# Retention and HGRN2 step on one core: low parts of W_out's B11 behind a scan's update, one scan step a product later, 17 small matmuls made twice

## The chip, the cores and the metric

The kernel runs on one core of a Trainium2 chip. The metric is the device time of one execution in microseconds (us); several runs are given by their median. One further execution was taken with a profile; all rows below are of that one.

The engines are called as the profile calls them: PE is TensorE's array and PEld its weight loads, DVE is VectorE, ACT is ScalarE, POOL is GpSimd, SP is SyncE (here it issues DMAs only). A matmul's output lies in PSUM; every other tile lies in SBUF.

## The reference, cut to what matters

One layer with two groups of four heads on the same normalised input of 2048 tokens by 1024 features: retention with a fixed decay for each head, and HGRN2, whose decay differs for each token and feature. Both are recurrences, taken in chunks; the outputs are gated and go together through one projection. Eight further tokens are decoded beside it.

```python
h = rmsnorm(x, norm_g)
p = (h @ w_in).astype(jnp.float32)
rq, rk, rv, rg, hq, hf, hi, hgate = jnp.split(p, 8, axis=-1)
...
# HGRN2: S_t = diag(f_t) S_{t-1} + k_t v_t^T, o_t = S_t^T q_t
b = jnp.cumsum(gc, axis=2)
o_inter = jnp.einsum('bhtd,bhdv->bhtv', qc * jnp.exp(b), S)
A = jnp.einsum('bhtd,bhsd,bhtsd->bhts', qc, kc, decay)
o = o_inter + jnp.einsum('bhts,bhsv->bhtv', A, vc)
...
o_cat = jnp.concatenate([o_ret, o_hg], axis=-1).astype(x.dtype)
y = x + o_cat @ w_out
```

The matrix `A` is the part that the change touches: its decay differs for each pair of tokens and each feature, so it isn't one product of q and k with a scalar in front.

## The kernel before

**Projections.** The products with W_in and W_out are cut into units, u from -6 to 31: values first (below 0), then W_in for queries, keys, forget gates and output gates (0 to 23), then W_out (24 to 31). By a scheme of Strassen's kind each unit is seven products of blocks (named by the operand of x: B11, T1, T2, B22, B21, T3, T4; operands of the weights are A11, S1 and so on), and each product is two halves of six matmuls, 128x512, at reduced precision: each operand is split into a high and a low part, and three of the four combinations are made. The high part is a rounding copy on ACT (`x_hi`, L743), the low part a subtraction on DVE (`x_lo`, L747), both over half of a block at a time; for x they are made once and kept for all units of the same half of the tokens. From unit 12 on the names begin with x1, for W_out with wo.

**Scans.** Units go round H (HGRN2: forget gates and queries), G (gates), R (retention: keys and queries). When a head's queries and forget gates are there, its scan is made beside the matmuls of the next units: unit 3's scan beside units 4 to 6, unit 9's beside units 10 and 11, unit 21's beside units 22 and 23. `A` is made by levels of a binary tree over the tokens. The steps `s0`, `s1`, `s2`, `s3` make the scores of one to two levels each, as runs of 32 fp32 matmuls of 32x16 (`small`, L1269; the first step also 32 of 32x32, L1287; the last step 16 of 32x32 and 16 of 32x64, L1321 and L1330). Between them DVE multiplies the keys and queries by the decay of a level (`update`: kh at L1234, then qth at L1237), and ACT copies them for the next step (`keep`: qh<-kh at L1248, fh<-qth at L1249), so that a step can make one level from the copies and the next level from the updated tiles. DVE puts the scores of the lower levels under a mask into fh (`put`, L1275); after the last step ACT copies the scores plh out of PSUM into A (L1340, L1342) and those of fh too (L1346). Then TensorE transposes the keys (pkh, L1085) and ACT copies them (ksh, L1091). The tiles pah, plh and pkh share one pool of two PSUM buffers: pkh's two groups take the buffers in which the last step's scores lay.

An fp32 matmul is two passes through the array, each with a weight load; so one fp32 matmul of a scan is four instructions of TensorE, and a 128x512 matmul of a product is two. `dec_mm(u)` (L809) are 16 fp32 matmuls for the decoded tokens on the weights of unit u.

**Order.** Nothing is reordered when the program is built: PE, DVE, ACT, POOL and SP each run their instructions in the order in which the code issues them. That order is set by an event list: `at(pos, f)` puts a piece of work at a position, where unit u's products stand at 7u and its next six slots, and the list is worked off by position. The table `AT` holds the offsets: `hgrn` for the scan's steps, `hd` for corrections to the steps of single scans (one tuple for each scan, offsets for s0 to s3), `swap` and `swapo` for the splits of x and of the operands of W_out, with four positions for each block (high and low part of its first half, then of its second). `wu` is the number of 32x8 matmuls on ones at the very start, ahead of the first product, which fill the time until its inputs have come.

## Time and profile before

| | us |
|---|---|
| median of 3 runs | 995.23 |
| the runs | 995.17, 995.23, 996.35 |
| the profiled execution | 994.56 |
| its span on the core | 992.8 |
| PE busy | 978.9 (99%) |
| DVE busy | 779.6 (79%) |
| ACT busy | 575.5 (58%) |
| POOL busy | 252.5 (25%) |
| mean DMA rate | 246 GB/s |

The span goes from the first to the last instruction on the core; 1.8 us of the execution's time lie around it. Busy times of engines overlap. An idle time in the profile is put down to what ended it: another engine's instruction, a DMA, or "issue", where the engine waited for nothing that the profile shows. TensorE's matmuls are pipelined, so that the starts of two matmuls lie closer together than one of them lasts. Runs of like instructions are given as one row with their count, and their passes are counted one by one. [...]

### The profile page before, as it was taken

How to read it: one execution, taken by the hardware profiler on the slowest of the kernel's cores; microseconds unless marked ns; L12 is line 12 of the kernel's file. 1: busy time of each engine (PE TensorE's matmuls, PEld its weight loads, DVE VectorE, ACT ScalarE, POOL GpSimd, SP SyncE). 2: the span in 40 equal slices, each digit the busy share in tenths (PEclk: the TensorE clock that was granted, in tenths of full speed). 3: DMA queues.
4: the chain of work that ended last, by engine and by line, in shares of the span. 5: the costliest groups of instructions: out<-in, count | busy, mean ns of one | idle time of the engine just before them, and what ended most of it. 6: DMA issues, size and time to landing. Idle time of an engine off the chain costs nothing. (4 is left out here: it accounts for less than half of the span.)

```text
span 992.8 us, 22960 instructions
## 1 busy us (share of the span) xinstructions
PE 978.9 (99%) x8831; PEld 815.9 (82%) x8831; DVE 779.6 (79%) x1355; ACT 575.5 (58%) x1348; POOL 252.5 (25%) x404
## 2 busy tenths in 40 slices
PE   9999999999999999999999999999999999999997
PEld 7788888888878887888888888888888878878886
DVE  6967696888778888878898766877867799867774
ACT  7855524856656664765885555456467577524332
POOL 1421231111332342232022222222237202312121
PEclk9999999999999999999999999999999999999999
DMA  9756669748868987784986993994996497784522
GB/s 310 239 182 245 223 218 360 291 154 301 261 194 279 300 284 266 269 273 159 354 277 187 320 307 121 317 303 130 317 333 215 156 362 275 244 267 156 212 85 85
DMA packets 121820, 244.05 MB, mean 246 GB/s; under 512 B 12600, under 2 KB 53184, under 8 KB 119024
## 3 DMA queue, kind: packets, MB, share of 16 engines
q1 hardware_dynamic: 98544, 164.69, 50.9%
q0 software_dynamic: 22880, 77.65, 21.1%
q8 instruction: 69, 1.13, 0.5%
q14 instruction: 39, 0.32, 0.1%
q10 hardware_dynamic: 288, 0.27, 0.1%
HBM read 155.97 MB, written 89.72 MB: 247 GB/s over the span
## 5 line engine op out<-in xcount | busy, mean ns | idle before, releaser
L1248 ACT ACTIVATE qh<-kh 128x1024 f32<-128x1024 f32 x24 | 25.5, 1062 | 46.3 <-DVE kh L1234 46.2
L1671 ACT ACTIVATE yj<-xro 128x512 f32<-128x512 f32 (+1 forms) x25 | 15.6, 624 | 60.3 <-DVE xro L750 42.7
L1234 DVE TENSOR_TENSOR kh<-kh,fph 128x512 f32<-128x512 f32 x48 | 33.0, 687 | 13.6 <-PE plh L1269 10.9
L1128 ACT ACTIVATE obh<-poh 128x128 f32<-128x128 f32 x64 | 16.9, 290 | 29.3 <-PE poh L1124 29.3
L1237 DVE TENSOR_TENSOR qth<-qth,fph 128x512 f32<-128x512 f32 x48 | 32.8, 683 | 0.0
L1128 ACT ACTIVATE obr<-por 128x128 f32<-128x128 f32 x64 | 16.8, 276 | 27.1 <-PE por L1124 27.1
L373 POOL TENSOR_TENSOR ms<-ms 128x2 f32<-128x2 f32 x8 | 10.0, 1255 | 86.5 <-ACT xn L369 86.5
L1689 DVE SCALAR_TENSOR_TENSOR xro<-xro,yms,fg 128x1024 f32<-128x1024 f32 (+1 forms) x16 | 20.0, 1247 | 13.5 <-POOL yms L1686 13.5
L1152 POOL DMA_DIRECT2D o_dram<-gtr x16 | 12.3, 769 | 67.5 <-DVE gtr L1149 20.8
L948 ACT ACTIVATE vo<-aV 128x512 f32<-128x512 f32 x12 | 7.1, 589 | 37.7 <-PE aV L918 37.7
L750 DVE TENSOR_TENSOR xro<-aO,xro 128x512 f32<-128x512 f32 (+1 forms) x33 | 22.2, 676 | 7.2 <-PE aO L918 7.1
L1152 POOL DMA_DIRECT2D o_dram<-gth x16 | 12.5, 778 | 57.5 <-DVE gth L1149 15.9
L265 POOL TENSOR_SCALAR orsh<-omsh 128x4 f32<-128x4 f32 x16 | 5.6, 347 | 83.3 <-ACT obh L1128 82.9
L1136 ACT ACTIVATE obh<-poh,orsh 128x128 f32<-128x128 f32 x64 | 18.2, 370 | 14.2 <-POOL orsh L266 14.2
L1115 DVE SCALAR_TENSOR_TENSOR sth<-sth,fph,puh 128x128 f32<-128x128 f32 x48 | 16.7, 347 | 10.3 <-PE poh L1124 7.8
L1122 PE MATMUL poh<-vh,A 128*128 128x128 f32 x128 | 24.0, 274 | 0.0
L1122 PE MATMUL por<-vr,A 128*128 128x128 f32 x128 | 24.0, 274 | 0.0
L1002 POOL DMA_DIRECT2D g_dram<-g x29 | 15.8, 546 | 27.8 <-DVE g L998 25.6
L1124 PE MATMUL por<-str,qr 128*128 128x128 f32 x112 | 21.8, 276 | 0.3 <-DVE str L1113 0.3
L369 ACT ACTIVATE xn<-xn 128x512 f32<-128x512 f32 x32 | 19.8, 622 | 3.5 <-DMA xn<-in_x_prompt 3.5
L1136 ACT ACTIVATE obr<-por,orsr 128x128 f32<-128x128 f32 x64 | 18.2, 368 | 6.1 <-POOL orsr L266 6.1
L1124 PE MATMUL poh<-sth,qth 128*128 128x128 f32 x112 | 21.7, 275 | 0.0
(1727 smaller groups left out, 3716.7 us busy)
## 6 DMA issues: line engine op xcount, KB each, us to landing
xn<-in_x_prompt SPq DMA_DIRECT2D x32, 256.0 KB, 4.4
v_dram<-vo SPq DMA_DIRECT2D x32, 256.0 KB, 2.4
xro<-in_x_prompt SPq DMA_DIRECT2D x16, 512.0 KB, 5.1
out_y_prompt<-xro POOLq DMA_DIRECT2D x15, 512.0 KB, 4.0
g_dram<-g POOLq DMA_DIRECT2D x29, 256.0 KB, 5.8
xr<-in_x_t SPq DMA_DIRECT2D x12, 512.0 KB, 6.2
vh<-v_dram SPq DMA_DIRECT2D x16, 256.0 KB, 8.8
gth<-g_dram SPq DMA_DIRECT2D x16, 256.0 KB, 6.7
```

Source lines behind the costliest of these rows:

```text
L369: act.activation(r, r, AF.Square, accum_out=ms[:, 2 * h + j : 2 * h + j + 1])
L750: dve.tensor_tensor(o, x, y, op=ALU.add)
L1115: dve.scalar_tensor_tensor(dst, src, decay(c), pu[:, j], op0=ALU.mult, op1=ALU.add)
L1122: pe.matmul(po[:, j], s_ctx["A"][:, c], box["v"][g][:, j], start=True, stop=src is None)
L1124: pe.matmul(po[:, j], qcol(c), src, start=False, stop=True)
L1128: act.activation(ob[:, j], po[:, j], AF.Square, accum_out=ms[:, j : j + 1])
L1136: act.activation(ob[:, j], po[:, j], AF.Copy, scale=rs[:, j : j + 1])
L1152: after(AT["gate"]["tr"], lambda: pool.dma_start(o_dram[c0 : c0 + 4, ty, :, h].rearrange("c p t -> p c t"), gt.rearrange("p (c t) -> p c t ...
L1234: dve.tensor_tensor(kv[:, :, 0, :], kv[:, :, 0, :], two[:, :, 1:2].to_broadcast([P, nb, b]), op=ALU.mult)
L1237: dve.tensor_tensor(qv[:, :, 1, :], qv[:, :, 1, :], two[:, :, 0:1].to_broadcast([P, nb, b]), op=ALU.mult)
L1248: act.activation(kept_k, k, AF.Copy)
L1689: dve.scalar_tensor_tensor(x[:, cc], x[:, cc], ms[:, 0:1], fg[:, cc], op0=ALU.mult, op1=ALU.mult)
```

## The change

Four things are edited.

- `swapo`'s B11, operand of W_out: high and low part of its second half stand 0.8 positions later. This moves them beside the scan of unit 21, behind its third step.
- `hd[3]`, the scan of unit 9: its third step `s2` stands a full position later, its last step `s3` 0.6 later. The third step now comes behind the product with B22 (eR<-x0B22) rather than ahead of it, and the last step between the two halves of the product with T3 (aR<-x0T3) rather than ahead of both.
- `wu`: 30 instead of 35; and `again`: after its 32 matmuls a scan step makes the first few again, with the same operands into the same place: 2 and 1 in the scan of unit 9 (s0, s2), 4 in unit 12's, 1 in unit 15's, 9 in unit 18's, 17 in all.
- `dec_mm(6)` stands just behind the third step of unit 3's scan, where it stood just ahead of it. Nothing else in TensorE's order there moves.

```diff
--- before.py
+++ after.py
@@ -115,7 +115,7 @@
            'lB21': 6.9,
            'lT3': 8.4,
            'lT4': 12.2,
-           'B11': (3.5, 3.5, 3.5, 3.5),
+           'B11': (3.5, 3.5, 4.3, 4.3),
            'T1': (6.5, 6.5, 7.0, 7.0),
            'T2': (8.2, 8.2, 8.7, 8.7),
            'B22': (8.9, 8.95, 9.2, 9.75),
@@ -126,7 +126,8 @@
  'x1s': (0.5, 1.8, 1.9, 3.4, 5.0),
  'wo': (26.9, 71.0, 101.8, 122.8),
  'wos': (0.0, 2.3, 3.3),
- 'wu': 35,
+ 'wu': 30,
+ 'again': {(3, 's0'): 2, (3, 's2'): 1, (4, 's2'): 4, (5, 's1'): 1, (6, 's2'): 9},
  'wop': (140.0, 2.133, 2.1, 2.833),
  'gate': {'G': 0.95, 'store': 1.6, 'R': 0.8, 'H': 0.7, 'root': 0.5, 'scale': 1.15, 'gt': 1.2, 'tr': 0.6},
  'fin': 1.0,
@@ -142,7 +143,7 @@
          'fin': 25.2},
  'dh': ((12.15, 14.75), (17.55, 20.15), (27.15, 28.65)),
  'dhs': (-5.0, -2.2, -2.2, -1.5),
- 'hd': ((0.0, 0.0, 0.0, 0.0), (0.0, 0.0, -0.5, -0.5), (0.0, 0.0, 0.0, 0.0), (0.3, 0.0, 0.0, 0.0),
+ 'hd': ((0.0, 0.0, 0.0, 0.0), (0.0, 0.0, -0.5, -0.5), (0.0, 0.0, 0.0, 0.0), (0.3, 0.0, 1.0, 0.6),
         (0.0, 0.0, 0.0, 0.0), (0.0, 0.5, 0.0, 0.0), (0.0, 0.0, 0.0, 0.0), (0.0, 0.0, 0.0, 0.5)),
  'retL': {'load': 12.0,
           's': 11.55,
@@ -831,8 +832,8 @@
         for n, name in enumerate(("A11", "S3", "A22", "A12")):
             at(U + {0: -7.6, 1: -8.6}.get(u, AT["w24"][0] if u == 24 else w["load"] if u % 3 or u >= 12 else w["load0"]) + 0.5 * n, lambda name=name: w_load(u, name))
         if u < 12:
-            if u == 3:
-                at(AT["hgrn"]["s2"] + AT["hd"][0][2] + 0.01, lambda: dec_mm(u))
+            if u in (3, 6):
+                at(7 * (u - 3) + AT["hgrn"]["s2"] + AT["hd"][u // 3 - 1][2] + 0.01, lambda: dec_mm(u))
             else:
                 at(U + d["mm" if u % 3 or not u else "mm0"], lambda: dec_mm(u))
             at(U + (-0.65 if u < 2 else d["copy" if u % 3 else "copy0"]), lambda: dec_copy(u))
@@ -1253,20 +1254,23 @@
             after(0.35, copies)
             after(1.1, lambda: update(li))
 
-        def small(dst, li, kept=False):
+        def small(dst, li, kept=False, again=0):
             b = LEVELS[li]
             m = 32 // (2 * b)
-            for c in range(CH):
-                for i in range(4):
-                    at_ = c * P + 32 * i
-                    if not kept:
-                        kk = k[:, at_ : at_ + 32]
-                        n0 = (c * 4 + i) * m
-                        qq = views(b)[0][:, n0 : n0 + m, 1, :]
-                    else:
-                        kk = kept_k[:, at_ : at_ + 32]
-                        qq = kept_q[:, at_ // 2 : at_ // 2 + 16]
-                    pe.matmul(dst[32 * i : 32 * i + 32, c], kk, qq, start=True, stop=True)
+            for n in range(4 * CH + again):
+                c, i = divmod(n % (4 * CH), 4)
+                at_ = c * P + 32 * i
+                if not kept:
+                    kk = k[:, at_ : at_ + 32]
+                    n0 = (c * 4 + i) * m
+                    qq = views(b)[0][:, n0 : n0 + m, 1, :]
+                else:
+                    kk = kept_k[:, at_ : at_ + 32]
+                    qq = kept_q[:, at_ // 2 : at_ // 2 + 16]
+                pe.matmul(dst[32 * i : 32 * i + 32, c], kk, qq, start=True, stop=True)
+
+        def more(step):
+            return AT["again"].get((u // 3, step), 0)
 
         def put(src, li):
             b = LEVELS[li]
@@ -1285,7 +1289,7 @@
                 for i in range(4):
                     cc = slice(c * P + 32 * i, c * P + 32 * i + 32)
                     pe.matmul(pd[32 * i : 32 * i + 32, c], k[:, cc], q[:, cc], start=True, stop=True)
-            small(p0, 0)
+            small(p0, 0, again=more("s0"))
             update(0)
             products(0, 1)
             keep(1)
@@ -1300,7 +1304,7 @@
         def scores(li):
             pl = ps_lv.tile([P, 2, CH, 16], F32, tag="lv", name=f"pl{name}{li}")
             small(pl[:, 0], li, True)
-            small(pl[:, 1], li + 1)
+            small(pl[:, 1], li + 1, again=more("s1" if li == 1 else "s2"))
             update(li + 1)
             keep(li + 2)
```

The order that comes of it, first on ACT beside the scan of unit 9. kh and qth are the scan's keys and queries, kr a tile of keys of the retention unit beside it (sw and big take its halves crosswise), x1T1l and x1T1h the low and high part of T1 of the second half of the tokens. Before:

```order
L1248 ACTIVATE qh_4783<-kh_4983 128x1024
L1249 ACTIVATE fh_4744<-qth_5117 128x512
L1009 ACTIVATE sw_5676<-kr_5406 64x512
L1010 ACTIVATE sw_5676<-kr_5406 64x512
L743 ACTIVATE x1T1h<-x1T1l 128x1024
L1340 ACTIVATE A<-plh_5681 32x4x32 x4
L1342 ACTIVATE A<-plh_5682 64x4x64 x2
L1346 ACTIVATE A<-fh_4744 32x8x32 x4
L743 ACTIVATE x1T1h<-x1T1l 128x1024
L1009 ACTIVATE big<-kr_5406 64x512
L1010 ACTIVATE big<-kr_5406 64x512
```

And after:

```order
L1249 ACTIVATE qh_4778<-kh_4978 128x1024
L1250 ACTIVATE fh_4739<-qth_5112 128x512
L1010 ACTIVATE sw_5672<-kr_5403 64x512
L1011 ACTIVATE sw_5672<-kr_5403 64x512
L744 ACTIVATE x1T1h<-x1T1l 128x1024 x2
L1010 ACTIVATE big<-kr_5403 64x512
L1011 ACTIVATE big<-kr_5403 64x512
L1344 ACTIVATE A<-plh_5690 32x4x32 x4
L1346 ACTIVATE A<-plh_5691 64x4x64 x2
L1350 ACTIVATE A<-fh_4739 32x8x32 x4
```

Both high parts of x1T1 and both copies into big now stand ahead of the copies of scores into A; what comes behind these, ksh, is the same in both.

Next DVE beside the scan of unit 21, from the gates' g on; r24S is an operand of W_out's first unit. Before:

```order
L998 SCALAR_TENSOR_TENSOR g_9582<-g_9582,pk,big 128x512
L747 TENSOR_TENSOR woB11l<-woB11l,woB11h 128x1024 x2
L1234 TENSOR_TENSOR kh_9045<-kh_9045,fph_9416 128x32x16
L1237 TENSOR_TENSOR qth_9178<-qth_9178,fph_9416 128x32x16
L1275 COPY_PREDICATED fh_8835<-lmask,plh_9609 128x16x8
L1275 COPY_PREDICATED fh_8835<-lmask,plh_9609 128x8x16
L750 TENSOR_TENSOR kr_9443<-eR_9457,kr_9443 128x512
L762 TENSOR_TENSOR r24S_9701<-r24S_9465,r24A_9553 128x512
```

And after:

```order
L999 SCALAR_TENSOR_TENSOR g_9594<-g_9594,pk,big 128x512
L748 TENSOR_TENSOR woB11l<-woB11l,woB11h 128x1024
L1235 TENSOR_TENSOR kh_9057<-kh_9057,fph_9428 128x32x16
L1238 TENSOR_TENSOR qth_9190<-qth_9190,fph_9428 128x32x16
L1279 COPY_PREDICATED fh_8847<-lmask,plh_9619 128x16x8
L1279 COPY_PREDICATED fh_8847<-lmask,plh_9619 128x8x16
L748 TENSOR_TENSOR woB11l<-woB11l,woB11h 128x1024
L751 TENSOR_TENSOR kr_9455<-eR_9469,kr_9455 128x512
L763 TENSOR_TENSOR r24S_9713<-r24S_9477,r24A_9565 128x512
```

The second low part of woB11 moved from ahead of kh's update to behind the two masked copies, ahead of kr<-eR. On ACT its high part moved from behind the first one to behind qh<-kh and fh<-qth. Beside unit 9's scan DVE's kr<-eR moved ahead of the update of kh, and one subtraction of x1T1l ahead of the last update. The orders of POOL and of SP are unchanged.

## Rows read from the trace of the kernel before

**Rows 1.** The page, busy time of each engine, its share and instructions.
```profile
PE 978.9 (99%) x8831; PEld 815.9 (82%) x8831; DVE 779.6 (79%) x1355; ACT 575.5 (58%) x1348; POOL 252.5 (25%) x404
```

**Rows 2.** TensorE's waits over the span: what ended them, total, times, longest.
```profile
PE plh L1269 <- issue: 3.4, 2, 2.5
PE bG L918 <- issue: 1.1, 1, 1.1
```

**Rows 3.** Timeline of PE: start, us, operation, count, [idle before <- what ended it].
```profile
290.32 0.40 PE L918 MATMUL bG<-x0B21l,w4A 128*128 128x512 f32 x1 [1.14 <-issue]
290.55 0.62 PE L918 MATMUL bG<-x0B21h,w4A 128*128 128x512 f32 x2
...
394.81 0.44 PE L1269 MATMUL plh<-qth,kh 128*32 128x16 f32 x31 [2.46 <-issue]
...
799.70 0.32 PE L1269 MATMUL plh<-qth,kh 128*32 128x16 f32 x15 [0.97 <-issue]
```

**Rows 4.** The page, DMA queues: packets, MB, share of 16 engines.
```profile
q8 instruction: 69, 1.13, 0.5%
```

**Rows 5.** Stretches: length, busy us and count by engine, PEclk, DMA share, GB/s.
```profile
284.00:290.30 6.30, 5.17 (x171) 4.04 (x170) 3.48 (x6) 1.90 (x5) 0.00 (x0) 1.00 0.50 183
290.31:394.80 104.49, 102.04 (x1274) 85.66 (x1274) 88.00 (x161) 62.52 (x149) 33.31 (x56) 1.00 0.81 271
386.50:394.80 8.30, 5.86 (x145) 4.34 (x145) 4.83 (x9) 3.76 (x6) 0.68 (x2) 1.00 1.02 388
394.81:799.68 404.87, 403.49 (x4444) 342.03 (x4443) 319.30 (x589) 254.84 (x621) 113.42 (x160) 1.00 0.77 255
```

**Rows 6.** DMA packets of queue 8 in 392.4 to 392.7, then in 797.3 to 797.6.
```profile
q8 instruction: 1, 0.02, 21.4%
...
q8 instruction: 1, 0.02, 20.2%
```

**Rows 7.** Timeline of PE beside unit 9's scan.
```profile
475.33 0.70 PE L1269 MATMUL plh<-fh,qh 128*32 128x16 f32 x62
...
486.76 0.48 PE L918 MATMUL aH<-x1B11h,w12A 128*128 128x512 f32 x1
```

**Rows 8.** Timeline of DVE in unit 3's third scan step.
```profile
306.25 0.68 DVE L1237 TENSOR_TENSOR qth<-qth,fph 128x512 f32<-128x512 f32 x1
```

**Rows 9.** Timeline of PE in unit 3's third scan step.
```profile
306.45 0.30 PE L809 MATMUL pdp<-r6A,xz 128*32 128x128 f32 x2
...
307.34 0.73 PE L1269 MATMUL plh<-fh,qh 128*32 128x16 f32 x62
307.90 0.19 PE L1269 MATMUL plh<-qth,kh 128*32 128x16 f32 x1
```

**Rows 10.** Timeline of ACT in unit 9's scan.
```profile
478.90 1.06 ACT L1248 ACTIVATE qh<-kh 128x1024 f32<-128x1024 f32 x1 [2.04 <-DVE kh L1234]
479.86 0.61 ACT L1249 ACTIVATE fh<-qth 128x512 f32<-128x512 f32 x1
...
481.27 0.63 ACT L1010 ACTIVATE sw<-kr 64x512 f32<-64x512 f32 x1
481.93 1.06 ACT L743 ACTIVATE x1T1h<-x1T1l 128x1024 fp32r<-128x1024 f32 x1
482.89 1.09 ACT L1340 ACTIVATE A<-plh 32x128 f32<-32x128 f32 x4
484.00 0.77 ACT L1342 ACTIVATE A<-plh 64x256 f32<-64x256 f32 x2
```

**Rows 11.** Timeline of DVE in unit 21's scan.
```profile
798.45 2.35 DVE L747 TENSOR_TENSOR woB11l<-woB11l,woB11h 128x1024 fp32r<-128x1024 f32 x2
...
803.07 0.69 DVE L750 TENSOR_TENSOR kr<-eR,kr 128x512 f32<-128x512 f32 x1 [0.53 <-ACT fh L1249]
...
808.49 0.68 DVE L1234 TENSOR_TENSOR kh<-kh,fph 128x512 f32<-128x512 f32 x1
```

**Rows 12.** Timeline of PE in unit 21's scan.
```profile
809.35 1.03 PE L1085 MATMUL pkh<-ident,kh 128*128 128x128 f32 x8
```

## Prediction, made before the changed kernel was run

> **What bounds the kernel now.** The page's first part comes first: TensorE is busy in 99% of the span [rows 1], so whatever TensorE loses the end loses, and what DVE, ACT or a DMA does counts only where TensorE stands still for it. So the second view is TensorE's waits [rows 2]: three idle times end in "issue", 3.4 us in two places and 1.1 us in one, and no other engine holds it in them. The timeline shows them [rows 3]: 1.14 us at 290.32 between two matmuls of a product, 2.46 us at 394.81 and 0.97 us at 799.70, each in the middle of a scan step's run of small matmuls: together 4.57 us.
>
> I read them as the arrival of instructions. Queue 8 carries instructions in 69 packets of 1.13 MB together [rows 4], 16.4 KB each; TensorE's 17,662 matmuls and weight loads [rows 1] with its other instructions make about 17,820, and a 69th of that is 258, so a packet holds 256 instructions or nearly. Between the first gap and the second lie 1274 matmuls and 1274 loads [rows 5] and, in the program's order, 12 semaphore instructions: 2560, ten times 256. Between the second and third lie 4444, 4443 and 73: 8960, 35 times 256. And a queue 8 packet runs at 392.4 to 392.7 and another at 797.3 to 797.6 [rows 6], 2.3 us before TensorE goes on at 394.81 and at 799.70. [...]
>
> **Shift of the block ends.** An fp32 matmul of the scan is two passes, each with its weight load: four instructions. Five warm-ups fewer at the start put every block end 20 instructions later in the program. (The warm-ups themselves lie ahead of the first product, which waits for its inputs: I cost their removal at nothing.) The repeats take that back step by step: 12 after the fourth scan's first step, 8 after its third, then 8 the other way, 12, and 48 before the scan of unit 21.
> - First gap. The block before it holds 63 passes of the diagonal scores, 64 of the first level and one long matmul. [...] The gap goes: −1.14.
> - But not all of that is kept. In unit 3's third scan step TensorE's second half needs DVE's update of qth, which ends at 306.93 [rows 8]; TensorE comes to it at 307.90 [rows 9], 0.97 late. Without the gap it comes 1.14 earlier, and the 16 decode matmuls ahead, which take 0.89 us from 306.45 on [rows 9], now stand behind the step: it would be there at 305.9, and waits until about 306.6, some 0.7 us (DVE's own chain in between was started by the product behind the gap, so it moves up by 0.3 to 0.4). Net −0.4; ends −1.14 (DVE moves up with it) and 0.
> - Second gap. The block before it has 25 decode passes, 6 long matmuls and 97 scan passes. Moved by 20 instructions it loses 10 decode passes for 10 scan passes, and its end still lies within the same run of small matmuls. [...] I take 0: the gap stays at 2.46. [...]
> - Third gap. There the shift is 48 the other way: the block gets nine long matmuls more, 2 us against a gap of 0.97. It goes, three in four; what that is worth is seen below.
> - The 17 repeats themselves: 17 × 17 ns = +0.3.
> - Elsewhere some six blocks that end in scan steps get shorter by up to 1 us. None gives a gap now; I take 0 and leave 0 to +1.5.
>
> **Fourth scan (unit 9).** Its third step (the change's "second step" of later scores) goes behind one product, 2.8 us later, and the last step into the middle of the next. TensorE loses nothing by that alone. The chain is ACT's, which works in program order. Now ACT copies kh at 478.90, then qth, turns kr round in two copies, makes one high part of T1, and at 482.89 copies the scores out of PSUM [rows 10]; TensorE's transposes of kh need the two PSUM tiles that these copies free by 484.8, over 1 us before they run, and the next product starts behind them at 486.76 [rows 7]. In the order of the changed kernel ACT has, between the copy of qth and that of the scores, both high parts of T1 and both copies into big. By rows: the third step ends on TensorE at 479.4, DVE's update of kh follows, so ACT's kh copy starts at about 480.2 instead of 478.90; then 0.96 for it, 0.55 for qth, 2 × 0.64 for the turn, 2 × 0.96 for T1, 2 × 0.64 for big [rows 10] (each the distance of two starts, or 0.64 for a copy of kr's half, big's like the turn's): the score copies start at 486.2, 3.3 us later than now. The first four take 1.11, the next two 0.7 [rows 10]: the second tile is free at 488.0, half of the transposes, eight of which take 1.03 [rows 12], follow, and the product that now starts at 486.76 starts at 488.5. **+1.75.** Ends +0.5 (ACT gets its T1 and big inputs without a gap and the transposes need only the first tile) and +2.
>
> **B11 of W_out beside the scan of unit 21.** Now DVE makes both low parts in a run at 798.45, 2.35 us for the two, ahead of the update of kh [rows 11]. The change puts the second half behind the update and the copies of masked scores, and its high part on ACT behind the copies of kh and qth. So the update starts some 1.1 earlier, at 799.6; ACT's copy of qth, for which kr<-eR waits now at 803.07 [rows 11], ends 1.1 earlier too, at 801.9, and ACT's second high part takes 0.96 from there, to 802.85. DVE, done with the masked copies at 801.4, waits for it: low part from 802.9 to 804.0, and only then kr<-eR. From there DVE runs without a break to the last update of kh, which now starts at 808.49, and TensorE's transposes start behind it at 809.35 [rows 11, 12]. So that update comes 0.94 later, and TensorE's transposes with it; they were bound by it, with under 0.2 us to spare. +0.8 against now. The third gap's 0.97, if it goes, is eaten here: TensorE then waits 1.75 instead of standing 0.97 earlier. Ends −0.97 (DVE catches up, the gap's gain is kept) and +1.2 (the gap stays too).
>
> **Sum.** −0.4 + 0 + 0.3 + 1.75 + 0.8 = +2.45. The profiled execution took 994.56; the changed kernel's would take 997.0. The median of the runs, 995.23, lies 0.67 above the profiled one, so 997.7. That is 0.25% above, just outside the 0.2% (2 us) that a measurement of this kernel can tell from no change.
>
> **Rivals.**
> - All block ends fall well (faster). [...] If the request for the block at 394.81 meets an emptier queue, all three gaps go, −4.57 + 0.3 = −4.3: 991.0; each wait behind them (0.7 in unit 3, 1.75 in unit 9, 1.75 in unit 21) that bites takes its part back. It decides for faster while less than 2.3 us of those is given back, so 991 to 993.2. For it: the gaps are the only idle time worth naming, and two of the shifts do lengthen the block. Against: the second block isn't longer, and ACT's order in unit 9 is fixed. 0.17.
> - Gains and waits even out (no difference): either the second gap goes and the waits come as worked out, 2.45 − 2.46: 995.2; or it stays and the waits in units 9 and 21 come at half, 995.5 to 997. 0.36.
> [...]
> - The shift does nothing (the gaps are not blocks, or follow the data, not the count): the waits alone, 0.3 + 1.75 + 0.8: 998.1. Against it: both counts are whole multiples of 256. 0.06. [...]
>
> **How the numbers follow.** The forecast as summed, with its own range of 997.2 to 998.9, has 0.24; with new gaps 0.17 and no effect of the shift 0.06 slower has 0.47; no difference 0.36; faster 0.17. The range of 992.8 to 1000.3 reaches into the faster rival and takes in most of the new gaps, leaving about 0.1 at each end.
>
> **What would show it.** In the changed kernel's waits: "issue" at bG<-x0B21l of unit 4 gone; at plh<-qth of unit 6 still 2 us or more; at plh<-qth of unit 21 gone. At unit 3's third step a wait for DVE's qth of about 0.7 us. Ahead of aH of unit 12 a wait of pkh for ACT's A copies of 1.5 to 2 us, with ACT's score copies behind big. At unit 21 pkh waiting for kh by about 1.7 us, and DVE idle before the second woB11l. Wrong if the gap in unit 6 goes, if pkh of unit 9 doesn't wait, or if any "issue" over 0.5 us stands in a new place.

## The result, and the profile after

The changed kernel took 999.67 us in the median of 5 runs (999.01 to 1001.19), the kernel before 995.17 in 5 runs beside them (993.69 to 996.35). The ratio is 1.0046, with a 95% interval of 1.0031 to 1.0061: **slower by 4.5 us**, more than the 0.2% below which it could not be told from no change. The forecast was 997.7 and slower; the time lies inside the range, 2 us above the forecast.

The profiled execution took 999.67 us with a span of 997.9, that of before 994.56 with 992.8: 5.1 us of span to account for. TensorE is still what counts: busy 981.7 us instead of the 978.9 of [rows 1], in 8855 passes instead of 8831, 24 more: two for each of the 17 repeats, less two for each of the five warm-ups.

The page of the changed kernel, busy time by engine:

```profile
PE 981.7 (98%) x8855; PEld 817.9 (82%) x8855; DVE 779.9 (78%) x1355; ACT 575.8 (58%) x1348; POOL 247.5 (25%) x404
```

TensorE's waits over the span of the changed kernel (what ended them, total us, times, longest), to be held against [rows 2]:

```profile
PE plh L1270 <- issue: 3.3, 2, 2.7
PE pkh L1086 <- DVE kh L1235: 1.4, 1, 1.4
...
PE plh L1270 <- DVE qth L1238: 1.1, 2, 0.7
PE pkh L1086 <- ACT A L1344: 0.8, 1, 0.8
PE plh L1334 <- DVE qth L1238: 0.7, 2, 0.3
PE pdp L810 <- DMA r0A<-in_w_in: 0.5, 1, 0.5
```

Of the three waits for "issue" (4.5 us) one is left, that of unit 6; those at bG of unit 4 and in unit 21 are gone. The second of the two that now make 3.3 us is new and stands in unit 18. In place of the gaps that went stand waits for DVE and ACT that are new or longer: of pkh, TensorE's transposes of kh, and of plh, the scan's scores.

The timeline of TensorE in the changed kernel at the places that the prediction named (start, us, operation, count, idle time before it and what ended that):

```profile
306.29 0.70 PE L1270 MATMUL plh<-qth,kh 128*32 128x16 f32 x62 [0.66 <-DVE qth L1238]
...
394.42 0.37 PE L1270 MATMUL plh<-qth,kh 128*32 128x16 f32 x21 [2.67 <-issue]
395.53 1.05 PE L919 MATMUL eR<-x0B22h,w8S 128*128 128x512 f32 x2
...
485.54 0.72 PE L1334 MATMUL plh<-qth,kh 128*32 128x64 f32 x32 [0.33 <-DVE qth L1238]
...
488.68 1.45 PE L1086 MATMUL pkh<-ident,kh 128*128 128x128 f32 x8 [0.82 <-ACT A L1344]
489.88 0.48 PE L919 MATMUL aH<-x1B11h,w12A 128*128 128x512 f32 x1
...
714.68 0.32 PE L1270 MATMUL plh<-qth,kh 128*32 128x16 f32 x17 [0.58 <-issue]
...
810.86 0.65 PE L1334 MATMUL plh<-qth,kh 128*32 128x64 f32 x32 [0.33 <-DVE qth L1238]
814.47 1.06 PE L1086 MATMUL pkh<-ident,kh 128*128 128x128 f32 x8 [1.37 <-DVE kh L1235]
```

Packets of queue 8 in the changed kernel, as in [rows 6], in 392.0 to 392.3 and in 712.2 to 712.5:

```profile
q8 instruction: 1, 0.02, 20.9%
...
q8 instruction: 1, 0.02, 20.3%
```

Each stands 2.3 to 2.4 us ahead of where TensorE goes on, at 394.42 and at 714.68. The gap of unit 6 shows what a block end is: [rows 3] has 31 passes left behind it, here 21 are left. Five warm-ups of four instructions are missing in front, so the end lies 20 instructions, ten passes, later in the program; the gap moved along with it within the same run, and did not go.

**Where the 5.1 us are.** I set the start of each long matmul in the changed kernel against the start of the same one in the kernel before; what the difference gains or loses over a stretch is that stretch's:

| stretch | us | made of | predicted |
|---|---|---|---|
| start to 269 us | +0.65 | a wait of 0.45 for a DMA (r0A, decode) and small things | 0 |
| 269 to 288 us | −0.88 | the eleven other kernels gain 0.4 to 0.9 here too: before's was long | 0 |
| unit 4's gap and unit 3's third step | −0.48 | −1.30 gap, +0.82 given back (wait 0.66 for qth) | −0.4 |
| unit 6's gap | +1.81 | gap 2.67 for 2.46, and +1.56 at half clock behind it | 0 |
| fourth scan, unit 9 | +2.02 | waits 0.33 and 0.82, transposes 1.45 for 1.03, small things | +1.75 |
| units 12 to 18 | +1.1 | new gap 0.58, repeats 0.24 by the prediction's price, 0.3 not placed | 0 to +1.5, repeats |
| unit 21 | +0.92 | −1.13 gap, then +0.49 and +1.56 (waits 0.33 and 1.37) | +0.8 |
| from there to the end | −0.05 | | 0 |

Sum +5.09.

**The clock behind unit 6's gap.** Three stretches of the changed kernel from the gap on (length; busy us and count of PE, PEld, DVE, ACT, POOL; PEclk, the granted clock as a share of full speed; DMA share; GB/s):

```profile
394.42:395.00 0.58, 0.58 (x22) 0.55 (x22) 0.15 (x1) 0.00 (x0) 0.22 (x1) 1.00 1.07 418
395.00:398.60 3.60, 3.60 (x10) 2.78 (x10) 1.65 (x4) 2.26 (x4) 0.87 (x2) 0.53 0.97 376
398.60:402.00 3.40, 3.40 (x16) 2.51 (x14) 2.55 (x5) 1.79 (x3) 0.00 (x0) 1.00 0.11 41
```

In the kernel before, the stretch behind the same gap, with the same columns:

```profile
394.81:398.80 3.99, 3.99 (x47) 3.32 (x47) 2.28 (x5) 2.26 (x4) 1.84 (x3) 1.00 0.93 340
```

The granted clock was 0.53 in the mean of those 3.6 us, and for nearly all of that stretch the long matmuls started 0.43 us apart; before, it stayed at 1.00 and they started 0.23 apart. What TensorE did before it fell is the same in both: full work, a stand of 2.46 or 2.67 us, then the rest of the run of small matmuls.

**Unit 9.** ACT in the changed kernel, where the prediction read [rows 10] (same columns as TensorE's timeline):

```profile
481.29 1.06 ACT L1249 ACTIVATE qh<-kh 128x1024 f32<-128x1024 f32 x1 [3.26 <-DVE kh L1235]
...
484.19 2.01 ACT L744 ACTIVATE x1T1h<-x1T1l 128x1024 fp32r<-128x1024 f32 x2
486.22 0.63 ACT L1010 ACTIVATE big<-kr 64x512 f32<-64x512 f32 x1
486.87 0.63 ACT L1011 ACTIVATE big<-kr 64x512 f32<-64x512 f32 x1
487.52 1.10 ACT L1344 ACTIVATE A<-plh 32x128 f32<-32x128 f32 x4
488.65 0.77 ACT L1346 ACTIVATE A<-plh 64x256 f32<-64x256 f32 x2
```

The order is the one expected: both parts of T1 and both copies into big now stand between the copies of kh and qth and those of the scores. From the kh copy to the first score copy are 6.23 us (481.29 to 487.52), 3.99 before (478.90 to 482.89); the next product starts at 489.88 instead of 486.76, of which some 1.1 is what had been lost further up. Within the transposes TensorE stands once more, for the second tile; the second half of them in TensorE's timeline from 489.4 on:

```profile
489.47 0.66 PE L1086 MATMUL pkh<-ident,kh 128*128 128x128 f32 x4
```

ACT is done with that tile at 489.42 (488.65 and 0.77), and the product follows 0.46 later.

**Unit 21.** DVE in the changed kernel, where the prediction read [rows 11]:

```profile
802.67 1.22 DVE L748 TENSOR_TENSOR woB11l<-woB11l,woB11h 128x1024 fp32r<-128x1024 f32 x1
...
807.09 1.23 DVE L748 TENSOR_TENSOR woB11l<-woB11l,woB11h 128x1024 fp32r<-128x1024 f32 x1 [1.44 <-ACT woB11h L744]
808.23 0.68 DVE L751 TENSOR_TENSOR kr<-eR,kr 128x512 f32<-128x512 f32 x1
...
813.64 0.69 DVE L1235 TENSOR_TENSOR kh<-kh,fph 128x512 f32<-128x512 f32 x1
```

DVE's two low parts are apart now, and it stands 1.44 us for ACT's high part before the second. The last update of kh comes at 813.64 and TensorE's transposes wait 1.37 for it.

### The profile page after: what moved, and what is told of

It reads as the page before. It is cut to its first block, busy times and chain, and to the rows that moved or that the text cites. A ratio compares the mean times of both kernels' runs of the same rounds, so it can differ in the third digit from the quotient of the medians.

```text
span 997.9 us, 23006 instructions
## 1 busy us (share of the span) xinstructions
PE 981.7 (98%) x8855; PEld 817.9 (82%) x8855; DVE 779.9 (78%) x1355; ACT 575.8 (58%) x1348; POOL 247.5 (25%) x404
## 5 line engine op out<-in xcount | busy, mean ns | idle before, releaser
L374 POOL TENSOR_TENSOR ms<-ms 128x2 f32<-128x2 f32 x8 | 5.2, 654 | 90.9 <-ACT xn L370 90.9
```

## The experiments

The theory after the result: the two moves cost what ACT's and DVE's order says, some 3 us together; the shift of the block ends takes gaps away in one place and makes others. The rival: the moves cost little, and the loss comes from the shift alone, or from how long TensorE is kept busy at the start. All eleven kernels, in the order of the sections below (median, that of the kernel before beside it, ratio with its 95% interval):

| kernel | us | before | ratio |
|---|---|---|---|
| 30 warm-ups alone | 1000.64 | 996.32 | 1.0049 [1.0027, 1.0071] |
| changed, fourth scan put back | 998.54 | 996.32 | 1.0026 [1.0013, 1.0039] |
| changed, B11 put back | 998.06 | 996.32 | 1.0025 [1.0000, 1.0051] |
| the two moves alone | 997.65 | 996.32 | 1.0022 [1.0011, 1.0033] |
| changed, both moves put back | 997.38 | 995.07 | 1.0017 [0.9999, 1.0035] |
| 33 warm-ups alone | 994.78 | 995.07 | one run |
| 25 warm-ups alone | 1000.41 | 995.07 | one run |
| idle matmuls to place the block ends | 998.51 | 995.07 | 1.0023 [1.0005, 1.0041] |
| scan steps thinned out | 1001.82 | 996.52 | 1.0053 [1.0034, 1.0071] |
| changed, high part of T1 later | 999.48 | 996.52 | 1.0039 [1.0025, 1.0054] |
| changed, other warm-ups | 999.79 | 995.95 | 1.0048 [1.0025, 1.0070] |

None of them is faster than the kernel before by more than its runs scatter.

### The shift alone

```diff
- 'wu': 35,
+ 'wu': 30,
```

> The kernel before with 30 warm-up matmuls instead of 35 and nothing else, so that only the ends of the 256-instruction blocks move, by 20 instructions. If the gaps are block ends: the gap of 1.14 us at bG<-x0B21l of unit 4 goes; the one at plh<-qth of unit 6 stays, 2.4 to 2.8 us, and the ten matmuls behind it run at half clock as in the changed kernel (+1.5); the third moves within the last scan and may grow, 0.5 to 2.3. Time 995 to 998. Rival, gaps follow the data and not the count: the three gaps stand where they stood, 1.14, 2.46 and 0.97, time within 0.5 of the kernel before. Second question: if fewer warm-ups bring the wait of pdp for r0A's load at 164 us (0.45), it appears here; if that is chance, it may not.

Measured: 1000.64, ratio 1.0049. TensorE's waits for instructions in this kernel's timeline:

```profile
227.06 0.28 PE L1269 MATMUL plh<-qth,kh 128*32 128x16 f32 x11 [1.11 <-issue]
...
396.67 0.51 PE L1269 MATMUL plh<-qth,kh 128*32 128x16 f32 x21 [2.61 <-issue]
...
805.98 0.30 PE L1269 MATMUL plh<-qth,kh 128*32 128x16 f32 x5 [2.70 <-issue]
```

The gap in unit 4 is gone, as worked out, the one in unit 6 has 21 passes left, exactly as in the changed kernel, and a new one stands at 227 us. The gap in unit 21 became longer by 1.7 us: it is the repeats, 48 instructions the other way, that took it away in the changed kernel. The expectation was missed on the high side. The changed kernel's wait for r0A (0.45) isn't there, and the moves alone, with 35 warm-ups, have 0.37 of it: it does not come from the fewer warm-ups. In the profile, two stretches at half clock stand behind the gaps of unit 6 (+2.6 us) and unit 21 (+1.25 us), and the first products after the warm-ups started 0.43 us apart instead of 0.23 (+1.6 us). The stretch behind unit 6's gap (columns as above):

```profile
396.67:400.70 4.03, 4.03 (x30) 3.22 (x30) 1.81 (x4) 2.26 (x4) 1.09 (x2) 0.50 0.96 372
```

Over the 9 runs the mean granted clock was 0.9952, over the 25 of the kernel before 0.9973. Within those 25, a run with a clock lower by 0.001 took about 1.5 us more (a straight line through the 25 pairs), so about 3 of the 4.3 us between the medians go with the clock; that the clock is their cause isn't shown by this.

### Either move put back, and the moves alone

Fourth scan put back in the changed kernel:

```diff
- 'hd': ((0.0, 0.0, 0.0, 0.0), (0.0, 0.0, -0.5, -0.5), (0.0, 0.0, 0.0, 0.0), (0.3, 0.0, 1.0, 0.6),
+ 'hd': ((0.0, 0.0, 0.0, 0.0), (0.0, 0.0, -0.5, -0.5), (0.0, 0.0, 0.0, 0.0), (0.3, 0.0, 0.0, 0.0),
```

> The changed kernel with the fourth scan's steps back where they were before. By my theory unit 9's scan costs 2.0 us in the changed kernel (pkh waits 0.82 for ACT's score copies, its second half some more, and plh 0.33 for qth): all of it goes, time 1.7 to 2.1 below the changed kernel, 997.6 or so. Rival: TensorE would have lost that time anyway at the next place (transfers or DVE late beside units 11 and 12): less than 0.7 below.

B11 put back in the changed kernel:

```diff
-           'B11': (3.5, 3.5, 4.3, 4.3),
+           'B11': (3.5, 3.5, 3.5, 3.5),
```

> The changed kernel with all of W_out's B11 made at the old place. By my theory the waits of plh for qth (0.33) and of pkh for kh (1.37) at unit 21 go and the gap of 0.97 stays away, so 1.7 to 1.9 below the changed kernel, 997.8. Rival: the gap at unit 21 comes back with the old order (0.97) or pkh waits anyway since DVE cannot be earlier: 0 to 0.9 below.

The kernel before with the two moves and nothing else of the change:

```diff
-           'B11': (3.5, 3.5, 3.5, 3.5),
+           'B11': (3.5, 3.5, 4.3, 4.3),
- 'hd': ((0.0, 0.0, 0.0, 0.0), (0.0, 0.0, -0.5, -0.5), (0.0, 0.0, 0.0, 0.0), (0.3, 0.0, 0.0, 0.0),
+ 'hd': ((0.0, 0.0, 0.0, 0.0), (0.0, 0.0, -0.5, -0.5), (0.0, 0.0, 0.0, 0.0), (0.3, 0.0, 1.0, 0.6),
```

> The kernel before with the two moves alone (fourth scan, W_out's B11); warm-ups, repeats and decode matmuls as before, so block ends stay up to unit 9. By my theory: first gap 1.14 and second gap 2.46 as before, full clock behind both; unit 9 +2.0; unit 21 +0.8 to +1.2 on top of the kernel before: 2.8 to 3.2 above it, 998.1. Rival: the moves are free and the loss is all the shift's (half clock behind the second gap, a new gap in unit 18): within 0.7 of the kernel before.

Measured: 998.54, 998.06 and 997.65. With the fourth scan put back, both waits in unit 9 are gone, and in the profile its stretch is as long as in the kernel before, where the changed kernel loses 2.02. The ratio falls from 1.0046 to 1.0026, about 2 us, though the two intervals overlap. With B11 put back the wait of pkh in unit 21 is 0.28 instead of 1.37, and the stretch of unit 21 is 1.4 us shorter:

```profile
PE pkh L1086 <- DVE kh L1235: 0.3, 1, 0.3
```

The gap there stays away, and of the 1.1 us that this is worth 0.49 is kept up to the end of the stretch. The moves alone, with the blocks where they were, bring back both waits. TensorE's waits in that kernel:

```profile
PE pkh L1085 <- DVE kh L1234: 1.2, 1, 1.2
...
PE pkh L1085 <- ACT A L1340: 0.9, 1, 0.9
```

Its three old gaps are there too (1.52, 1.88 and 1.02 us), and one of 0.65 at 233 us. Its ratio says +2.2 (1.1 to 3.3) where the two stretches show 1.9 and 1.4 in the profile: the sizes of the moves lie at the upper end of the interval. And the clock did not fall behind its gap in unit 6, of 1.88 us with 31 passes left (columns as above):

```profile
396.12:400.10 3.98, 3.98 (x47) 3.34 (x47) 2.29 (x5) 2.27 (x4) 1.84 (x3) 1.00 0.98 368
```

### The changed kernel without both moves

```diff
-           'B11': (3.5, 3.5, 4.3, 4.3),
+           'B11': (3.5, 3.5, 3.5, 3.5),
- 'hd': ((0.0, 0.0, 0.0, 0.0), (0.0, 0.0, -0.5, -0.5), (0.0, 0.0, 0.0, 0.0), (0.3, 0.0, 1.0, 0.6),
+ 'hd': ((0.0, 0.0, 0.0, 0.0), (0.0, 0.0, -0.5, -0.5), (0.0, 0.0, 0.0, 0.0), (0.3, 0.0, 0.0, 0.0),
```

> The changed kernel with both moves taken back: 30 warm-ups, 17 repeats and the decode matmuls behind unit 3's step remain. If the parts add up: changed minus 2.0 (fourth scan) minus 1.6 (B11), so about 1 above the kernel before: gap at unit 4 gone with 0.65 given back, gap at unit 6 with half clock behind it (+1.5), gap at unit 21 gone, 0.5 or so new in unit 18. Rival: with both moves gone the shift gains what it was sized for, 2 or more below the kernel before.

Measured: 997.38, ratio 1.0017, so +1.7 (−0.1 to 3.5). The shift and the repeats by themselves gain nothing: the gaps of units 4 and 21 are gone, and TensorE's waits for instructions in this kernel are

```profile
225.81 0.28 PE L1270 MATMUL plh<-qth,kh 128*32 128x16 f32 x11 [1.20 <-issue]
...
396.08 0.51 PE L1270 MATMUL plh<-qth,kh 128*32 128x16 f32 x21 [2.47 <-issue]
...
714.24 0.33 PE L1270 MATMUL plh<-qth,kh 128*32 128x16 f32 x17 [0.65 <-issue]
```

4.32 us, against 4.57 before, with half clock behind the second (long matmuls 0.43 us apart, 0.23 before) and a wait of 0.65 for qth at 307.43 where the gap of unit 4 went. The moves alone (+2.2) and this kernel (+1.7) add up to 3.9, the whole measured 4.5; the intervals cover the difference.

### Other numbers of warm-ups

```diff
- 'wu': 35,
+ 'wu': 33,
```

> The kernel before with 33 warm-ups: block ends 8 instructions later. By my theory the gap at unit 4 shrinks to 0.6 or less, since its block gains four long matmuls less than with 20 instructions, and the one at unit 6 ends with some 27 passes left instead of 31, 2.2 to 3 us long. Which way the clock goes behind it I don't know: full with 31 passes left in two kernels, half with 21 in four; if the length of the gap decides, it should fall when the gap is over 2.5. Time 995 to 997.

and the same with 25:

> The kernel before with 25 warm-ups: block ends 40 instructions later. By my theory no gap at unit 4 (its block then holds 17 long matmuls), a gap at unit 6 of 2.5 to 3 us with 11 passes left behind it, and one each of 0.5 to 2 us in the scans of units 15, 18 and 21, where blocks get shorter than 5.1 us; half clock behind the long ones. Time 997 to 1001. Rival: the gaps stay where they were.

Measured in one run each: 994.78, within the 23 runs of the kernel before beside it (992.20 to 998.59), and 1000.41, above all of them. With 33, the three gaps are 0.52, 2.31 and 1.72 us (4.55 in all) with 27 passes left in unit 6; with 25 the gap of unit 4 is gone and four gaps, that of unit 6 among them, make 9.3. TensorE's timeline with 25 warm-ups:

```profile
228.06 0.21 PE L1269 MATMUL plh<-qth,kh 128*32 128x16 f32 x2 [3.42 <-issue]
...
397.80 0.30 PE L1269 MATMUL plh<-qth,kh 128*32 128x16 f32 x11 [2.38 <-issue]
...
561.41 0.33 PE L1269 MATMUL plh<-qth,kh 128*32 128x16 f32 x17 [2.47 <-issue]
...
806.92 0.73 PE L918 MATMUL eR<-x1B22h,w23S 128*128 128x512 f32 x2 [1.05 <-issue]
```

The passes left in unit 6 read 31, 27, 21 and 11 with 35, 33, 30 and 25 warm-ups: four passes of two instructions for two warm-ups, ten passes for five, twenty for ten. **A block end moves by four instructions for each warm-up matmul: the gaps follow the count of instructions.** The other profiles bear it out. The thirteen of them hold 29 idle times of TensorE over 0.5 us that end in "issue". Counted through TensorE's instructions in the trace (matmuls, weight loads and those for semaphores), every one of the 29 stands behind a number of instructions that leaves 193 when divided by 256, and a packet of queue 8 begins 2.3 to 3.0 us before TensorE goes on. So the gaps stand at ends of blocks of 256 instructions, about what a packet of queue 8 holds (some 17,820 in 69 packets in the kernel before). That TensorE waits there for the next block is the author's reading of these numbers; how long ahead of its use a block is asked for, no run shows. The gap itself is 2.46, 2.31, 2.61 and 2.38 in these kernels: moving the end within the run changes it little. Behind 11 passes left the clock stayed at 1.00 for the 4 us that followed, and so it did behind the three other gaps with 25 warm-ups, where half clock was expected behind the long ones. That blocks under 5.1 us stall was the author's estimate, and no run shows it as a limit: in the kernel before, blocks of 1.53, 2.64, 3.54, 3.81 and 4.11 us have no gap behind them. The length of the gap doesn't decide either: behind 2.31 us (33 warm-ups) the clock stayed (0.999 in the mean of that execution), behind 2.23 us (fourth scan put back) it fell (long matmuls 0.43 us apart).

### Block ends placed by hand

73 matmuls of 32 x 8 elements, written into PSUM tiles that real matmuls then overwrite, so that block ends fall into products (33 warm-ups besides):

```diff
- 'wu': 35,
+ 'wu': 33, 'fill': {'dec7': 14, 'dec8': 13, 'dec10': 16, 'dec11': 15, 'o140': 10, 'o160': 5},
+    def fill(t, key):
+        for n in range(AT["fill"].get(key, 0)):
+            pe.matmul(t[32 * (n % 4) :][:32, :8], ones[:, :32], ones[:, :8], start=True, stop=True)
...
+        dec["pt"] = ps_o.tile([P, P], F32, tag="o", name=f"pdp{u}"); fill(dec["pt"], f"dec{u}")
...
+            po = ps_o.tile([P, 4, P], F32, tag="o", name=f"po{name}{g}"); fill(po[:, 0], f"o{half}{hd}{g}")
```

> The kernel before, no move at all, with 33 warm-ups and 73 idle 32x8 matmuls put ahead of decode matmuls (units 7, 8, 10, 11) and ahead of two heads' outputs, into PSUM that the next matmul overwrites: only block ends move, scan by scan, to places where the block before an end holds long matmuls too. By my theory of the blocks: the gaps of 2.46 (unit 6) and 0.97 (unit 21) go, the one of 1.14 (unit 4) shrinks to 0.6 or less, none over 0.8 comes elsewhere; the fills cost 73 x 17 ns = 1.2: 3 below the kernel before, 992.2 (991 to 993.5). Rival, requests are late whatever the block holds: gaps of the same total at new places, 995 to 997.

Measured: 998.51 over 12 runs (993.62 to 1000.93), ratio 1.0023; the expectation was missed, and it is the rival that came, gaps of the same total at new places. In its profile the three old gaps are gone, and one new one takes nearly all of their 4.57 us:

```profile
559.61 0.51 PE L1272 MATMUL plh<-qth,kh 128*32 128x16 f32 x20 [4.17 <-issue]
```

with half clock behind it (0.994 in the mean of that execution, 0.999 in the profiled one of before), and a wait of 1.76 us for a DMA of the decode weights at 390 us. Moving the ends out of three places put one into a fourth.

### Blocks with fewer small matmuls

If it is the density of tiny matmuls in a block, then thinning them out should remove gaps wherever the ends fall: half of the passes of the two middle scan steps half a product earlier, with 27 warm-ups and 85 idle matmuls for the places that were left. How long a block has to last to pass without a gap was the author's estimate, and no run shows it; from it the waits for instructions were put at under 2 us in sum, and the time at 1 to 3 us below the kernel before.

```diff
- 'wu': 35,
+ 'wu': 27, 'kh': 0.5, 'fill': {'dec7': 17, 'dec8': 16, 'dec11': 2, 'o070': 10, 'o140': 15, 'o141': 15, 'o160': 10},
...
+        def kept_half(li):
+            pl = half_done[li] = ps_lv.tile([P, 2, CH, 16], F32, tag="lv", name=f"pl{name}{li}")
+            small(pl[:, 0], li, True)
...
+            if n in ("s1", "s2"):
+                at(7 * u + pos - AT["kh"], lambda n=n: do("h" + n[1]))
```

> The kernel before, with the half of a scan's middle steps that reads ACT's copies half a product earlier, so that six long matmuls stand between the two runs of small ones, and with 27 warm-ups and 85 idle 32x8 matmuls to put block ends well, scan by scan. [...]

Measured: 1001.82, ratio 1.0053: the slowest of all. Yet its waits for instructions are the shortest of all the kernels, under 2 us as expected:

```profile
PE plh L1272 <- ACT fh L1252: 1.8, 2, 1.4
PE pdp L812 <- DMA r9A<-in_w_in: 1.7, 1, 1.7
PE plh L1272 <- issue: 1.2, 1, 1.2
```

1.2 us against 4.57. That fits the density as the cause of the gaps, but doesn't show it apart, since the idle matmuls chose the block ends as well. Thinning the steps out cost more than it brought, and the time expected did not come: 16 more changes between a run of small matmuls and the long ones of a product took about 0.36 us each (each step's own extra time, from the starts of the long matmuls around it), 5.8 us in all, and ACT's and the decode's waits came in addition.

### Unit 9 without its wait for ACT

If pkh waits because ACT makes both high parts of T1 ahead of the score copies, putting the second one 0.2 positions later, behind them, ends the wait:

```diff
-           'T1': (6.0, 6.0, 6.5, 6.5),
+           'T1': (6.0, 6.0, 6.7, 6.7),
```

> The changed kernel with the high part of T1's second half 0.2 positions later (all units' order else the same): on ACT it then stands behind the copies of scores into A beside unit 9's scan. If ACT's place in that order is what holds pkh there, the score copies start 1 us earlier, pkh's wait of 0.82 goes to under 0.2, and aH of unit 12 starts 0.8 to 1 earlier against its neighbours: 0.9 below the changed kernel. Rival, pkh is held by DVE's update of kh or by the PSUM tiles of fh's copies: the wait stays.

Measured: the wait is gone. TensorE's transposes in this kernel stand without an idle time ahead:

```profile
491.44 1.45 PE L1086 MATMUL pkh<-ident,kh 128*128 128x128 f32 x8
```

and ACT makes the second part of T1 behind the score copies:

```profile
490.28 1.11 ACT L1344 ACTIVATE A<-plh 32x128 f32<-32x128 f32 x4
491.41 0.77 ACT L1346 ACTIVATE A<-plh 64x256 f32<-64x256 f32 x2
...
493.79 1.06 ACT L744 ACTIVATE x1T1h<-x1T1l 128x1024 fp32r<-128x1024 f32 x1
```

The step up to aH of unit 12 lost 0.65 us instead of 1.52, 0.87 less, as expected. So ACT's order was the cause of that part. The median, 999.48 with a ratio of 1.0039, is 0.7 us nearer to before by the ratios, but the intervals overlap widely. The transposes still take 1.45: the second tile is free only at 492.18 (491.41 and 0.77), 0.74 behind the first transpose.

### Warm-ups of another kind

The same number of instructions at the start, but more of the long warm-ups and fewer short ones, so that the block ends stay where they are in the changed kernel and TensorE is busy longer ahead of the first product:

```diff
- 'wu': 30,
+ 'wu': 28,
-    for n in range(7):
+    for n in range(9):
```

> The changed kernel with two more of the long warm-up matmuls (9 of 128x128 instead of 7) and two short ones fewer (28 instead of 30), so that the same number of instructions, and so the same block ends, lie ahead of the first product, but TensorE is kept busy 0.8 us longer. If fewer warm-ups let the clock fall at the start of some executions (as in three of eight profiles with 30 or fewer, whose first matmuls start 0.43 us apart instead of 0.23), all executions start at full speed here, the mean granted clock rises from 0.997 to 0.998, and the time is 0.3 to 1.5 below the changed kernel. Rival: the first product waits for its inputs in any case and the early clock is chance: no difference, or up to 0.6 more where the warm-ups now run past the inputs.

Measured: 999.79 (ratio 1.0048), the changed kernel's time; the clock over the 11 runs was 0.9968. The expected gain did not come, and the first product started at 6.13 us instead of 5.37. The gap in unit 6 (2.63 us, 21 passes left), half clock behind it (long matmuls 0.43 us apart), and the waits in units 9 and 21 (1.07 and 1.36) are as in the changed kernel. Keeping TensorE busy at the start doesn't bring the loss back, and in the changed kernel's own profile none has arisen there: at 160 us its long matmuls start 0.04 us earlier than before's.

## Why the prediction was right, and where it was not

**The moves: right in kind, close in size.** Unit 9 was put at +1.75 and took 2.02; the route was ACT's order, as the prediction wrote it, and T1 taken out of the way removed the wait. The mis-sized term is ACT's chain: from its kh copy to the score copies the prediction adds up 6.0 us (480.2 to 486.2) where 6.23 came, and the last two score copies took 0.77 for 0.7. The transposes were sized rightly: the product starts 0.46 behind the second tile, where half of 1.03 was put. The wait itself was expected in one piece of 1.5 to 2 us and came in three: 0.33 for qth, 0.82 ahead of the transposes, some 0.3 inside them. Unit 21 was put at +0.8 and took +0.92: the gap's gain of 1.13 eaten, TensorE waiting 0.33 for qth and 1.37 for kh where about 1.7 was expected, DVE idle 1.44 ahead of the second low part, as foreseen. The moves alone measured 2.2 (1.1 to 3.3), somewhat less than the 2.55 of the two terms.

**First gap: right.** −0.4 predicted, −0.48 found, by a wait of 0.66 for DVE's qth where 0.7 was expected. That it is the move of `dec_mm(6)` that gives so much back can be read from other profiles: in the six kernels with that move in which this gap goes, the stretch gains 0.46 to 0.49, in the three without it and with the scan steps as before (30 and 25 warm-ups alone, block ends by hand) 0.60 to 0.87.

**Second gap: right that it stays, wrong on what it costs.** The step "I take 0: the gap stays at 2.46" held (2.67, and 2.2 to 2.6 in six other kernels at this place with 21 passes left). No run shows how long ahead of its use a block is asked for, and this 0 and the −1.14 of the first gap rested on the author's estimate of it; the runs showed the first gap at 1.14, 0.52 and twice none, and the second at 2.46, 2.31, 2.61 and 2.38, with 35, 33, 30 and 25 warm-ups. The packet began at 392.1, 0.3 us later against the products around it than before, and 2.3 us ahead of TensorE as before. What failed is that nothing was counted behind the gap: TensorE's products there ran at half clock (granted 0.53 over 3.6 us), +1.56 us, and the prediction had no term for the clock. That the time lies in the range is at this place luck.

**Elsewhere: the part put at 0 to +1.5 was not nil.** Unit 18 has a new gap of 0.58, and the stretch costs 1.1. The block before that gap did not get shorter: counted as for the 29 gaps, it lasts 4.86 us up to the gap, and the same block of the kernel before, of 3.81 us, has none behind it. The repeats were taken at 17 ns a matmul, two passes, which is what the rows give (0.70 us for 62 passes [rows 7], less 0.18 for the last one's end); no run shows their cost apart. The prediction itself had named an "issue" over 0.5 us in a new place as what would make it wrong. The bound held, the value taken did not. With unit 6's gap this is nearly the whole of the miss: 1.81 there and 0.8 here, of the 2.64 between 5.09 and 2.45. Such a gap is no fixed property of the order: the kernels with 30 warm-ups have the same block ends up to unit 9, yet at 226 to 228 us three of them stand (1.11, 1.20 and 1.66 us, each with 11 passes left) and the changed kernel and three more do not, and the gap of unit 18 is there in two of the six that share the block ends up to it. One profile of a kernel thus shows one draw of its smaller gaps.

**How far the clock belongs to the change is not settled.** In the profile 1.56 us of it stands behind unit 6's gap. But the clock of the kernel before is lower in other executions too: its mean granted clock was 0.9973 to 0.9983 in the four sets of runs beside the experiments, the changed kernel's 0.9970 over its five runs, the profiled one of before 0.999. A difference of 0.0003 to 0.0013, at the 0.15 to 1.5 us per 0.001 that straight lines through the runs of before gave in the four sets, is 0 to 2 us. And after gaps of unit 6 with 21 passes left the clock fell in all seven profiles (long matmuls 0.43 us apart instead of 0.23), after those with 31, 31, 27 and 11 left in none; a gap of 3.42 us elsewhere (2 passes left) left it at 1.00. Neither the length of the gap nor the count of passes behind it alone decides. What does stays open. The mechanism was not isolated: no run changed the clock alone.

**The rivals.** "Gains and waits even out", the likeliest of them at 0.36, came in neither form: the second gap stayed, and the waits of units 9 and 21 came in full. New gaps, given 0.17, came in one place, the 0.58 of unit 18. "All block ends fall well" fell with the gap in unit 6. "The shift does nothing" is refuted: block ends moved by four instructions per warm-up in four kernels. Nearly all block ends pass without a gap here, in number, yet the others are not cheap: one to four of about 70 took 1.2 to 9.3 us in the kernels with shifted ends. Which ones stalled changed with where the ends fell, and the one at 226 to 228 us stalled in three of the seven kernels that share it.

**Why the gaps that went brought little.** The two gaps that the change takes away (2.1 us) were paid back in place: 0.82 behind the first, and the third's 1.13 into waits that the moves opened. Only without the B11 move was part of the third one's gain kept (the stretch −0.49 instead of +0.92).

## What to carry to other kernels

Where a program is limited by one engine's instruction stream, an engine's idle time that ends in "issue" is a place to count instructions from, in both directions, to the next such place: whole multiples of one number show block ends (here 2560 and 8960, ten and 35 times 256). Moving one by a few instructions moved all those behind it here (each of the 29 gaps kept its 193), so a shift is to be judged by the sum of all gaps, and by what TensorE runs like behind each of them (a granted clock of 0.50 to 1.00 here). And before a step on the limiting engine is moved later, the orders of the engines that feed it should be written out up to its next use of their results, since a later start can let other work in ahead of them (here ACT's chain in unit 9 grew from 3.99 to 6.23 us).

## What the runs showed of the hardware that was not expected

- Behind gaps of 2.2 to 4.2 us the granted clock fell to half for some microseconds in nine places and did not in six others of similar length (1.88 to 3.42 us); in the three that were priced the cost was 1.25, 1.56 and 2.6 us.
- In the kernel with its scan steps thinned out, each change from a run of small fp32 matmuls to the 128x512 matmuls of a product and back took about 0.36 us, with nothing else waiting (16 more of them, 5.8 us).
- The first products after the warm-ups start 0.43 us apart in some executions and 0.23 in others, for the first few microseconds, while PEclk reads 1.00 in both: in that stretch the granted clock does not show it. Three of the thirteen profiles had it for 2 us or more (30 warm-ups alone, scan steps thinned out, T1 later), the changed kernel with the same 30 had not; what decides it stays open.
- The kernel before itself scatters from 991.8 to 1002.2 us over 80 runs, far wider than the three runs at the head of this document (995.17 to 996.35).
